# A fused diffusion-transformer step on one core: five fill groups ahead of the scan's first chunk in place of seven, and two 64-row copies that change engines

## The chip, the cores and the metric

One Trainium2 chip, one of its cores. The metric is the device time of one execution in microseconds (us), the median of several runs. Each of the core's engines works through its own queue of instructions in order: TensorE (PE in the profile; its weight loads are PEld), VectorE (DVE), ScalarE (ACT), GpSimd (POOL) and SyncE (SP), which issues all the DMA transfers of this kernel. They wait for each other by semaphores.

## The reference

One layer over 128 context tokens and 2048 latent tokens of width 1024, in 17 tiles of 128 tokens: a modulated RMSNorm; one projection; on one half of the heads a gated DeltaNet scan in both directions, on the other half a gMLP (gelu, layer norm, spatial mixing); an output projection with a gated residual; then a squared-ReLU MLP and a final norm. The part around the change is the scan with its triangular solve:

```python
a_mat = jnp.where(strict, jnp.einsum('bnhcd,bnhsd->bnhcs', k_beta, k) * decay, 0.0)
sol = lax.linalg.triangular_solve(a_mat + jnp.eye(DN_CHUNK), rhs, left_side=True, lower=True, unit_diagonal=True)

def step(S, xs):
    qd, kd, u_c, w_c, qk_c, gl = xs
    v_new = u_c - jnp.einsum('bhck,bhkv->bhcv', w_c, S)
    o = jnp.einsum('bhck,bhkv->bhcv', qd, S) + jnp.einsum('bhcs,bhsv->bhcv', qk_c, v_new)
    S = S * jnp.exp(gl)[..., None, None] + jnp.einsum('bhck,bhcv->bhkv', kd, v_new)
    return S, o
```

beside it `proj = h @ w_in`, of which the columns of the gate (g), of u and of vg (v) are computed here while the scan runs.

## The kernel before, in words

The program has three stages. The first projects q, k and v for all tiles and writes them to DRAM. The second, which the change touches, is the scan: 34 units (17 tiles, two directions), each a chunk of 128 tokens and four heads. The third is the MLP as one long row of matmuls.

In the scan each unit has a **prep** and a **chain**. The prep inverts a triangular matrix for four heads: a decay mask E (L1017, L1018 on ACT, two selections on POOL), the matrix KK (L1030 on DVE), its half-precision form AH (L1038 on ACT), a first X (L1039 on DVE), X transposed into Y (L1045 on PE, copied by L1047 on ACT). Then five levels of block size 2, 4, 8, 16, 32 follow. A level is a strict sequence over three engines: PE multiplies AH with Y (L1065), DVE copies the product under a mask into P (L1069), PE multiplies with P (L1076, L1079), ACT copies the new Y and X (L1080, L1081), and the next level can begin. The level of 64 rows is written apart: L1095 on PE, a copy Pm (L1097), L1103 and L1105 on PE, and the two copies Y (L1106) and X (L1107). L1113 and L1114 (PE) then read Y, their result goes through DVE into R (L1116), and L1122 (PE) reads X and R. The chain (L992, L1138, L1146, L1168, L1179, L1180) carries the state from unit to unit.

Since each prep step waits for the one ahead of it on another engine, PE is kept busy with **fills** between the steps. Fills are the 51 groups (17 tiles, g, v and u) of the second projection: a group is 24 matmuls of 128x512 (L224, L225, L226: a product in three parts over eight k), cut by `PARTS` into pieces of 9, 9 and 6 matmuls, followed by its gelu or gate on ACT and DVE (L1214 to L1274). The gate of a tile from the fifth on writes a buffer `gw` of which there is one, and stores it to DRAM (L1246); the next writer of `gw` waits for that store. Later fills are the output projection and the first norm of the MLP (L863 is an eviction of that norm on ACT).

The order is set by hand: every step is given a time in units of chunks by `at`, the list `p2` (the first eight numbers of `WINDOWS`) says how far ahead of unit i its prep runs (from i - 2.46 to i - 0.03), where its chain lies, and between which times the fills of the second projection are spread (`p2[4]` to `p2[5]`). The first `NF` groups are not spread: they are put at time -12 or -8, ahead of the prep of the first unit. The steps are sorted by time and written out; within limits a scheduler then orders the instructions of each engine.

At times between -2 and -1.2 `split_next` also splits the weights of u into two parts (L195 on ACT, L196 on DVE), eight tiles that are loaded four at a time.

Of the kernel before, what the change touches and what calls it, by code (L numbers as in the profile page):

```python
# [31 lines left out]
def interleave(*lists):  # L32
# [5 lines left out]
    for _, _, _, s in sorted(order, key=lambda e: e[:3]):  # L38
# [8 lines left out]
NE = 4  # L47
LAG2 = 0
LAG3 = 3
NF = 7  # L50
LATE = 0.5
PARTS = ((0, 3), (3, 6), (6, 8))
PL = 0
# [5 lines left out]
NK = DFF // P // 2  # L59
AHEAD = 3  # L60
COMPUTE = (mybir.EngineType.DVE, mybir.EngineType.Activation, mybir.EngineType.Pool)
WINDOWS = [2.46, 0.03, -0.51, 1.06, -1.61, 18.16, 17.58, 18.3,
           2.63, -0.06, -0.18, 1.0, 1.36, 1.64, 1.66, 2.66, 3.17, 3.71]


# [1 line left out]
def hybrid_step(  # L67
# [7 lines left out]
    V, A, G, T = nc.vector, nc.scalar, nc.gpsimd, nc.tensor  # L75
# [209 lines left out]
    with ExitStack() as ph:  # L285
# [478 lines left out]
        for bi in range(len(BLOCKS)):  # L764
# [8 lines left out]
            for n, (gi, h) in enumerate(order):  # L773
                u = us[n] if bi == 0 and n < 3 else feature_tile(blk, bi, gi, h)
# [156 lines left out]
    with ExitStack() as ph:  # L931
# [8 lines left out]
        def pd():  # L940
            return psd.tile([P, 4, P], F32, tag="d", name="pd", bufs=4)
# [40 lines left out]
        def unit(t, d, fresh=False, last=False):  # L982

            u = {}
# [28 lines left out]
            @prep.append  # L1013
            def _():
                e = s32("E")
                for h in range(H):
                    A.activation(e[:, h, :], u["gb"][:, h, :], AF.Abs, scale=-1.0, bias=col(gcol, h))  # L1017
                A.activation(e, e, AF.Exp, scale=-1.0)  # L1018
                es = s32("Es")
                G.affine_select(out=es, in_=e, pattern=[[0, 4], [-sg, P]], compare_op=ALU.is_gt, fill=0.0,  # L1020
                                base=0, channel_multiplier=sg)
                G.affine_select(out=e, in_=e, pattern=[[0, 4], [sg, P]], compare_op=ALU.is_ge, fill=0.0,
                                base=0, channel_multiplier=-sg)
                u["Es"], u["E"] = es, e
# [64 lines left out]
            ra, rb = (lo, hi) if d == 0 else (hi, lo)  # L1089
# [9 lines left out]
            @prep.append  # L1099
            def _():  # L1100
                py, px = pd(), pd()
                for h in range(H):
                    T.matmul(py[ra, h, 0:64], u["X"][ra, h, ra], u["P"][ra, h, 0:64], start=True, stop=True)  # L1103
                for h in range(H):
                    T.matmul(px[rb, h, 0:64], u["P"][ra, h, 0:64], u["X"][ra, h, ra], start=True, stop=True)  # L1105
                V.tensor_copy(u["Y"][ra, :, rb], py[ra, :, 0:64])  # L1106
                A.copy(u["X"][rb, :, ra], px[rb, :, 0:64])  # L1107

            @prep.append
            def _():  # L1110
# [193 lines left out]
        def split_next(j):  # L1304
            n, k = wlist[j]
            if n != "u" and k == 0:
                ga1.append(wrow(mod_d[1:2, 2 * D + n * 512 : 2 * D + n * 512 + 512]))
                WO.append([])
            (W2 if n == "u" else WO)[n].append(split_w(wraw[j]))
            ahead()  # L1310
# [83 lines left out]
        def at(time, fn, kind=None):  # L1394
            events.append((time, len(events), fn, kind))
# [20 lines left out]

        p2, p3 = WINDOWS[:8], WINDOWS[8:]
        for i, u in enumerate(units):
# [35 lines left out]
        for key, _, st in flat:  # L1454
            if key < NF * KT:
                at(-8 if key >= HT * KT else -12, st)
# [4 lines left out]
        for j in range(len(wlist)):  # L1461
            at(-2 + 0.12 * j if j < KT else 16.4 + 0.12 * (j - KT), lambda j=j: split_next(j))
        flat = [e[1:] for e in flat if e[0] >= NF * KT]
        done, total = 0, sum(size for size, _ in flat)
# [440 lines left out]
    for p, (o, n, m) in enumerate(seq):  # L1905
        u = units[n]
# [117 lines left out]
```

## Time and profile before

| | |
|---|---|
| runs of the kernel before | 2613.35, 2617.05, 2619.66 us; median 2617.05 us |
| the profiled execution's own time | 2613.28 us |
| its span, first to last instruction | 2611.1 us |
| TensorE busy | 2563.6 us, 98% of the span |
| VectorE, ScalarE, GpSimd busy | 1765.4, 1242.2, 255.2 us |
| the scan's stage | from about 433 to 1242 us of the span |

The busy time of an engine says how full it is. Where TensorE is 98% busy, what is left to gain is its idle time and the time in which it runs at a lower granted clock (the column PEclk). In a list of waits, each row names the waiting instruction by engine, tile and line, then what ended the wait, then the sum in us, the number of waits and the longest. In the timeline a row is a start, a duration, engine, line, operation, and in brackets the idle time ahead of it with what ended it.

### The profile page before, as it was taken

Reading aid. Unit: us, or ns where it says so; the run is one execution under the profiler, and the core shown is the slowest. Engines: PE = TensorE matmul, PEld = TensorE weight load, DVE = VectorE, ACT = ScalarE, POOL = GpSimd, SP = SyncE. Lnnn points to the kernel's source line nnn. Section 1 sums busy time; section 2 is a strip of 40 time slices with the busy share of each in tenths; the row PEclk is TensorE's granted clock in tenths of the full one; section 3 lists DMA queues with packets and bytes.
Section 4 is the critical chain, followed back from the end, with each engine's and each line's share of the span. In section 5 each row is a group of like instructions: output and inputs, shape, how many; then the busy total and the mean of one; then the engine's idle time right before and its main releaser. Section 6 shows DMA issues by size and latency. Waiting matters only on the chain.

```text
span 2611.1 us, 44100 instructions
## 1 busy us (share of the span) xinstructions
PE 2563.6 (98%) x15330; PEld 2151.3 (82%) x15330; DVE 1765.4 (68%) x3587; ACT 1242.2 (48%) x3086; POOL 255.2 (10%) x478
## 2 busy tenths in 40 slices
PE   8999999899999999999999999999999999999998
PEld 4999999788888778878888888888887888888887
DVE  5867745666566777886588786677675544774874
ACT  4755555455555667774345653333342432242441
POOL 3112112111111122221000000000000000000000
PEclk9999999999999999999999999999999999999999
DMA  8967638645555667995778788445379978786773
GB/s 295 291 214 219 197 113 240 214 146 164 156 158 169 212 198 239 282 299 163 289 228 243 242 253 319 150 126 162 108 209 382 339 259 289 257 254 211 233 254 106
DMA packets 533860, 579.78 MB, mean 222 GB/s; under 512 B 35500, under 2 KB 366684, under 8 KB 530054
## 3 DMA queue, kind: packets, MB, share of 16 engines
q1 hardware_dynamic: 533638, 576.98, 69.4%
q8 instruction: 120, 1.97, 0.3%
q14 instruction: 102, 0.84, 0.1%
HBM read 397.62 MB, written 179.22 MB: 221 GB/s over the span
## 4 chain that ended last, share of the span: by engine, by line
PE 89%; DMA 4%; DVE 3%; ACT 2%; issue 1%; SPq 0%; POOL 0%; DVEq 0%; POOLq 0%; ACTq 0%
PE f L224 17%; PE f L226 16%; PE f L225 16%; PE pj L224 7%; PE pj L226 7%; PE pj L225 7%; PE pd L992 3%; PE pm L224 2%; PE pm L225 1%; PE pm L226 1%; PE pm L339 1%; PE pt L593 1%; PE pd L1179 1%; PE pd L1180 1%; PE pt L553 1%
## 5 line engine op out<-in xcount | busy, mean ns | idle before, releaser
L224 PE MATMUL f<-hop,zH 128*128 128x512 f32 x960 | 373.7, 390 | 2.0 <-ACT zH L1527 2.0
L226 PE MATMUL f<-hop,zL 128*128 128x512 f32 x960 | 373.6, 390 | 0.0
L225 PE MATMUL f<-hop,zH 128*128 128x512 f32 x960 | 373.2, 389 | 0.0
L224 PE MATMUL f<-hop,wH 128*128 128x512 f32 x896 | 351.5, 393 | 0.0
L225 PE MATMUL f<-hop,wH 128*128 128x512 f32 x896 | 348.9, 390 | 0.0
L226 PE MATMUL f<-hop,wL 128*128 128x512 f32 x896 | 344.0, 390 | 0.0
L1527 ACT CAST zH<-zraw 128x512 fp32r<-128x512 f32 x240 | 146.7, 620 | 282.5 <-DVE zraw L1521 86.1
L224 PEld LDWEIGHTS f<-hop,zH 128*128 128x128 f32 x960 | 180.2, 188 | 40.3 <-ACT zH L1527 3.2
L226 PEld LDWEIGHTS f<-hop,zL 128*128 128x128 f32 x960 | 180.2, 188 | 39.0 <-DVE zL L1521 1.6
L225 PEld LDWEIGHTS f<-hop,zH 128*128 128x128 f32 x960 | 180.2, 188 | 37.2
L1521 DVE TENSOR_TENSOR zL<-zraw,zH 128x512 fp32r<-128x512 f32 x240 | 162.4, 687 | 71.6 <-ACT zH L1527 54.6
L226 PEld LDWEIGHTS f<-hop,wL 128*128 128x128 f32 x896 | 168.2, 188 | 35.7
L224 PEld LDWEIGHTS f<-hop,wH 128*128 128x128 f32 x896 | 168.5, 188 | 34.2 <-issue 0.9
L225 PEld LDWEIGHTS f<-hop,wH 128*128 128x128 f32 x896 | 168.6, 188 | 32.2
L226 PE MATMUL pj<-kH,wL 128*128 128x386 f32 (+2 forms) x568 | 190.5, 335 | 0.0
L224 PE MATMUL pj<-kH,wH 128*128 128x386 f32 (+2 forms) x568 | 189.1, 335 | 0.3 <-DVE kH L491 0.3
L225 PE MATMUL pj<-kL,wH 128*128 128x386 f32 (+2 forms) x568 | 189.4, 333 | 0.0
L182 POOL TENSOR_TENSOR r<-rsq,nhalf 128x1 f32<-128x1 f32 (+1 forms) x38 | 22.8, 600 | 1386.2 <-DVE rsq L181 1386.2
L1674 ACT CAST wH<-s 128x512 fp32r<-128x512 f32 x96 | 58.9, 620 | 170.9 <-DVE s L1521 157.6
L1069 DVE CAST_PREDICATED P<-om,pd 128x256 f16<-128x256 uint16 x170 | 71.9, 427 | 99.7 <-PE pd L1065 99.4
L541 DVE SCALAR_TENSOR_TENSOR cv<-pj,vec,cv 128x384 f32<-128x384 f32 (+2 forms) x164 | 87.1, 539 | 56.2 <-ACT cv L538 54.9
L224 PEld LDWEIGHTS pj<-kH,wH 128*128 128x128 f32 x568 | 107.1, 189 | 4.6 <-issue 4.2
(410 smaller groups left out, 5871.1 us busy)
## 6 DMA issues: line engine op xcount, KB each, us to landing
zraw<-z_d SPq DMA_DIRECT2D x212, 256.0 KB, 4.5
raw<-in_w_ff_dram SPq DMA_DIRECT2D x128, 256.0 KB, 4.9
hop<-hop_d SPq DMA_DIRECT2D x28, 1024.0 KB, 14.0
z_d<-c SPq DMA_DIRECT2D x96, 256.0 KB, 2.5
zraw<-s_d SPq DMA_DIRECT2D x96, 256.0 KB, 5.2
raw<-in_w_mod_dram SPq DMA_DIRECT2D x80, 256.0 KB, 4.4
r<-in_w_ff_dram SPq DMA_DIRECT2D x80, 256.0 KB, 5.5
s_d<-s SPq DMA_DIRECT2D x64, 256.0 KB, 3.0
```

Source lines behind the costliest of these rows:

```text
L224: T.matmul(ps, lh, rh, start=first and i == 0, stop=False, skip_group_check=more)
L225: T.matmul(ps, lh, rl, start=False, stop=False, skip_group_check=more)
L226: T.matmul(ps, ll, rh, start=False, stop=last and i == n - 1, skip_group_check=more)
L339: T.matmul(pm[0:2, :], scond[:, k, :], raws[k], start=k == 0, stop=k == KT - 1)
L541: V.scalar_tensor_tensor(out=cv[:, o : o + m], in0=ps[:, s + sh : s + sh + m], scalar=convw[:, w, j : j + 1], in1=cv[:, o : o + m], op0=AL ...
L553: T.transpose(pq[:, i * P : (i + 1) * P], u["x2"][:, i * P : (i + 1) * P], ident)
L593: T.matmul(ps[:, i * P : (i + 1) * P], kTt[:, i * P : (i + 1) * P], rhs[:, i * P : (i + 1) * P], start=True, stop=True)
L992: T.matmul(p[:, h, :], lhs[:, h, :], rhs[:, h, :], start=True, stop=True)
L1069: V.copy_predicated(out=half(u["P"], yi), mask=half(bc4(om[s]).bitcast(U16), yi), data=pp)
L1521: V.tensor_tensor(out=out, in0=a, in1=b, op=op)
L1527: A.copy(h, src)
L1674: A.copy(h, s2)
```

## The change

`NF` goes from 7 to 5: ahead of the first unit stand the groups g of tiles 0 to 3 and of tile 4, and no longer g of tile 5 and v of tile 4, which become spread fills. The fills are spread from -2.1 in place of -1.61; their end (18.16) stays. And the two copies of the 64-row level change engines: Y goes from VectorE to ScalarE, X from ScalarE to VectorE. The work is the same, instruction for instruction.

```diff
-NF = 7
+NF = 5
...
-WINDOWS = [2.46, 0.03, -0.51, 1.06, -1.61, 18.16, 17.58, 18.3,
+WINDOWS = [2.46, 0.03, -0.51, 1.06, -2.1, 18.16, 17.58, 18.3,
            2.63, -0.06, -0.18, 1.0, 1.36, 1.64, 1.66, 2.66, 3.17, 3.71]
...
                 for h in range(H):
                     T.matmul(px[rb, h, 0:64], u["P"][ra, h, 0:64], u["X"][ra, h, ra], start=True, stop=True)
-                V.tensor_copy(u["Y"][ra, :, rb], py[ra, :, 0:64])
-                A.copy(u["X"][rb, :, ra], px[rb, :, 0:64])
+                A.copy(u["Y"][ra, :, rb], py[ra, :, 0:64])
+                V.tensor_copy(u["X"][rb, :, ra], px[rb, :, 0:64])
```

**Start of the scan on TensorE.** The first rows of unit 0, before:

```order
L226 MATMUL pj<-wH,hL 128x512
L1045 LDWEIGHTS X
L1045 MATMUL pd<-ident_179,X 128x128
...
L1065 LDWEIGHTS AH
L1065 MATMUL pd<-Y,AH 128x64
...
L1076 LDWEIGHTS X
L1076 MATMUL pd<-P_5734,X 128x64
```

and now, where `pm` is the product of group g of tile 5:

```order
L226 MATMUL pm<-wH,hL 128x512
L1045 LDWEIGHTS X
L1045 MATMUL pd<-ident_179,X 128x128
...
L224 MATMUL pm<-wH,hH 128x512
L225 MATMUL pm<-wL,hH 128x512
L226 MATMUL pm<-wH,hL 128x512
...
L1065 LDWEIGHTS AH
L1065 MATMUL pd<-Y,AH 128x64
```

Before, unit 0 goes from L1045 over L1065, L1076 and L1079 to the next L1065 with no fill in between, after all seven groups. Now 9 matmuls of the sixth group stand ahead of L1045, 9 behind it, 6 behind L1065, and then a piece of 9, 9 or 6 between each two steps of the first levels.

**Start of the scan on ScalarE and VectorE.** ScalarE from the first AH on, before:

```order
L1038 CAST AH<-KK 128x512
L1244 ACTIVATE gw<-pm 128x512
L195 CAST wH<-raw 128x512
L1047 CAST Y<-pd 128x512
L1244 ACTIVATE gw<-pm 128x512
L195 CAST wH<-raw 128x512 x2
L1080 CAST Y<-pd 128x128x2
L1081 CAST X<-pd 128x128x2
```

and now:

```order
L1047 CAST Y<-pd 128x512
L195 CAST wH<-raw 128x512
L1080 CAST Y<-pd 128x128x2
L1081 CAST X<-pd 128x128x2
L195 CAST wH<-raw 128x512 x2
L1017 ACTIVATE E<-gr,gcol 128x128 x4
L195 CAST wH<-raw 128x512
L1080 CAST Y<-pd 128x64x4
L1081 CAST X<-pd 128x64x4
L1018 ACTIVATE E<-E 128x512
L1244 ACTIVATE gw<-pm 128x512
```

The second gate that writes `gw` (the second L1244) stood between L1047 and the first L1080; it now stands behind the second level's copies. VectorE at the same place, now:

```order
L1069 COPY_PREDICATED P_5734<-om_186,pd 128x128x2
L1068 COPY P_5734<-identq 128x512
L196 TENSOR_TENSOR wL<-raw,wH 128x512 x2
L1069 COPY_PREDICATED P_5735<-om_187,pd 128x64x4
```

Two splits of weights (L196) stand ahead of the mask copy of the second level (P_5735); before there was one between these two mask copies on a tile of the same load, and one on a tile loaded earlier.

**The 64-row copies.** VectorE in the 19th unit, before:

```order
L1215 TENSOR_SCALAR gw<-gw 128x512
L1083 TENSOR_TENSOR QK<-QK,E 128x512
L1039 TENSOR_TENSOR X<-AH,sg_185 128x512
L1048 TENSOR_TENSOR AL<-KK,AH 128x512
L1106 CAST Y<-pd 64x4x64
```

and ScalarE in the same unit now:

```order
L1097 CAST Pm<-pd 64x4x64
L195 CAST wH<-raw 128x512
L1214 ACTIVATE gw<-pm 128x512
L1038 CAST AH<-KK 128x512
L1106 CAST Y<-pd 64x4x64
```

Y stands on ScalarE in the place that X had there (behind L1038), and X on VectorE in the place that Y had (behind L1048). In the units of the backward direction in which the norm's evictions run (L863, eight to a unit), ScalarE had, before, in one of them:

```order
L863 ACTIVATE ev<-pj,b_203,a_202 128x128 x4
L1038 CAST AH<-KK 128x512
L863 ACTIVATE ev<-pm,b_203,a_202 128x128 x4
L1107 CAST X<-pd 64x4x64
```

and has now:

```order
L863 ACTIVATE ev<-pj,b_203,a_202 128x128 x4
L1038 CAST AH<-KK 128x512
L863 ACTIVATE ev<-pm,b_203,a_202 128x128 x2
L1106 CAST Y<-pd 64x4x64
L863 ACTIVATE ev<-pm,b_203,a_202 128x128 x2
```

so that two of the eight evictions moved from ahead of the copy to behind it.

## The prediction

> **What bounds the kernel now.** I read the page first: the engines' busy time and the chain that ended last.
>
> ```profile
> PE 2563.6 (98%) x15330; PEld 2151.3 (82%) x15330; DVE 1765.4 (68%) x3587; ACT 1242.2 (48%) x3086; POOL 255.2 (10%) x478
> PE 89%; DMA 4%; DVE 3%; ACT 2%; issue 1%; SPq 0%; POOL 0%; DVEq 0%; POOLq 0%; ACTq 0%
> ```
>
> TensorE is the bound, and it has 2611.1 - 2563.6 = 47.5 us of idle time in all. The change removes no matmul, so it can gain only idle time and time at a low clock. The windows say where these lie (PE busy is the second number, PEclk the one ahead of the DMA share):
>
> ```profile
> 450.00:475.00 25.00, 21.95 (x109) 17.85 (x108) 7.16 (x14) 6.72 (x15) 1.92 (x3) 0.99 1.06 347
> 475.00:500.00 25.00, 21.68 (x155) 16.41 (x154) 15.24 (x45) 13.88 (x37) 3.88 (x5) 0.88 0.52 154
> sum 720.00, PE 700.08 PEld 579.80 DVE 501.17 ACT 420.50 POOL 124.39; mean PE 29.17 PEld 24.16 DVE 20.88 ACT 17.52 POOL 5.18
> ```
>
> The two stretches of 25 us at the scan's start hold 3.05 + 3.32 = 6.4 us of idle time, and 12% of the second is clock that was not granted. The sum is that of 600 to 1320 us: 19.9 us idle over the rest of the scan. The list of waits of TensorE over 430 to 1250 us names them:
>
> ```profile
> PE pd L1076 <- DVE P L1069: 12.9, 18, 2.2
> PE pd L1065 <- ACT Y L1080: 4.8, 6, 2.7
> PE pd L1113 <- DVE Y L1106: 4.5, 4, 2.2
> ```
>
> These are the largest of 27.8 us; all are prep steps that had too few fills ahead of them. The mean of a wait at L1076 is 12.9/18 = 0.72 us.
>
> **Term 1, the start of the scan.** TensorE's timeline there, and the three rows of its waits from 470 to 500 us:
>
> ```profile
> 470.64 0.39 PE L226 MATMUL pj<-wH,hL 128*128 128x512 f32 x1
> 470.87 0.40 PE L1045 MATMUL pd<-ident,X 128*128 128x128 f16 x4
> 471.94 0.28 PE L1065 MATMUL pd<-Y,AH 128*128 128x64 f16 x4 [0.67 <-ACT Y L1047]
> 472.75 0.28 PE L1076 MATMUL pd<-P,X 128*128 128x64 f16 x4 [0.53 <-DVE P L1069]
> 475.86 0.37 PE L1065 MATMUL pd<-Y,AH 128*128 128x64 f16 x4 [2.71 <-ACT Y L1080]
> 476.62 0.63 PE L225 MATMUL pj<-wL,hH 128*128 128x512 f32 x1
> 477.05 0.63 PE L226 MATMUL pj<-wH,hL 128*128 128x512 f32 x1
> 481.35 0.40 PE L226 MATMUL pj<-wH,hL 128*128 128x512 f32 x1
> ...
> PE pd L1076 <- DVE P L1069: 3.0, 3, 2.2
> PE pd L1065 <- ACT Y L1080: 2.7, 1, 2.7
> PE pd L1065 <- ACT Y L1047: 0.7, 1, 0.7
> ```
>
> The waits add up to 6.4 us. Behind the longest the clock halves: matmuls follow each other at 0.43 us (476.62, 477.05) where the full clock gives 0.228 (a group of 24 in 5.46 us). From 475.86 to about 481.1 us stand 10 of these and three sets of four small ones (some 0.12 each): 5.2 us for 2.6 us of work, so 2.6 us lost. The start costs 6.4 + 2.6 = 9.0 us.
>
> What the long wait hung on stands in the other queues (ScalarE, VectorE, SP, a piece of the chain); behind them are the groups by line over 430 to 1250 us, with the mean in ns, and one more row of ScalarE:
>
> ```profile
> 473.92 0.60 ACT L1244 ACTIVATE gw<-pm 128x512 f32<-128x512 f32 x1 [2.03 <-DMA gate_d<-gw]
> 475.44 0.37 ACT L1080 CAST Y<-pd 128x256 f16<-128x256 f32 x1
> 461.11 0.41 DVE L1039 TENSOR_TENSOR X<-AH,sg 128x512 f16<-128x512 f16 x1
> 463.75 1.07 SPq L188 DMA_DIRECT2D raw<-in_w_in_dram  x2
> 467.23 0.52 SPq L1004 DMA_DIRECT2D kT<-kT_d  x1
> 468.01 5.83 DMA gate_d<-gw
> ...
> L195 ACT CAST wH<-raw 128x512 fp32r<-128x512 f32 x31 | 18.8, 626 | 2.1 <-DMA raw<-in_w_in_dram 1.5 <-PE pm L226 0.5
> L196 DVE TENSOR_TENSOR wL<-raw,wH 128x512 fp32r<-128x512 f32 x32 | 21.8, 690 | 5.1 <-ACT wH L195 4.6 <-PE pm L226 0.4
> L1069 DVE CAST_PREDICATED P<-om,pd 128x256 f16<-128x256 uint16 x170 | 71.9, 427 | 99.7 <-PE pd L1065 99.4
> 497.20 1.28 ACT L1017 ACTIVATE E<-gr,gcol 128x128 f32<-128x128 f32 x4
> ```
>
> The second gate waits for the store of the one `gw` buffer (issued at 468.01, landed 5.83 us later), and L1080 is queued behind it on ScalarE. The order of the change puts that gate behind the second level's copies.
>
> Now the changed order, walked with these durations. Of the 48 matmuls that move, 9 stay ahead of L1045 and 39 go behind it, so TensorE reaches L1045 at 470.87 - 39 x 0.228 = 462.0, and X is ready at 461.5: no wait. L1045 takes 0.23 on the queue and 9 matmuls 2.05, which covers the copy to Y (0.6): L1065 at 464.3 without a wait. Six matmuls (1.37) cover the mask copy (0.43): L1076 at 465.8. Nine cover L1080 (0.37, now with one cast ahead of it that is done early): L1065 at 468.2. Nine more: L1076 at 470.4. Here **something else is late**. The mask copy of the second level now stands behind two weight splits whose tiles SP issues at 463.75 and about 464.3. By the 5.83 us from issue to landing they come at 469.5 and 470.1; each costs a cast on ScalarE (0.6) and a subtraction on VectorE (0.69), so the second is through at 471.5 and the mask copy at 471.9: a wait of 1.5 us. Next, ScalarE has four L1017 (1.28 for four) and a cast of the third tile ahead of the second L1080. That load now stands in SP's queue in the place of the kT load (467.23), so it lands at 473.0; cast and copy end at 474.0, while TensorE would be at L1065 at 473.6: a wait of 0.4. The steps behind these have 6 to 9 matmuls in front (1.37 to 2.05 us) and their engines free: 0.2 for all. I add one more open place at the mean of 0.72. **Left: 2.8; gain 9.0 - 2.8 = 6.2 us.** No idle stretch there is near the 4 us that stood before the half clock, so I leave no half clock in. Bounds: 9.0 if the loads land sooner than needed; 0 if they land 2 to 3 us later, since then the idle stretch and the half clock come back.
>
> On the clock, the Trainium skill (TensorE: Matmul & The Clock Gate, Part 1) says the clock halves after an idle window of about 3.4 us and comes back after a busy one as long. The 4 us of waits above agree; the second dip, in the next term, follows 2.4 us (1168.43 to 1170.83) that hold only eight small matmuls, so here the trace shows it sooner. By the page the left waits would be further from a dip; by the row they have some 0.9 us of room. The sum is the same by both.
>
> **Term 2, the 64-row copies.**
>
> ```profile
> L1106 DVE CAST Y<-pd x34: 405/422/429, 500.1 to 1234.2; 64x256 f16<-64x256 f32 x34
> L1107 ACT CAST X<-pd x34: 353/367/380, 500.1 to 1234.2; 64x256 f16<-64x256 f32 x34
> 903.91 0.36 ACT L1107 CAST X<-pd 64x256 f16<-64x256 f32 x1
> 905.80 0.43 DVE L1106 CAST Y<-pd 64x256 f16<-64x256 f32 x1
> 990.32 1.53 ACT L863 ACTIVATE ev<-pm,b,a 128x128 f32<-128x128 f32 x4
> 1168.76 0.36 ACT L1107 CAST X<-pd 64x256 f16<-64x256 f32 x1 [1.27 <-PE pd L1105]
> 1168.43 0.19 PE L1105 MATMUL pd<-X,Pm 64*64 64x64 f16 x1
> 1168.92 0.28 PE L1076 MATMUL pd<-P,X 128*128 128x64 f16 x4 [0.29 <-DVE P L1069]
> 1170.34 0.43 DVE L1106 CAST Y<-pd 64x256 f16<-64x256 f32 x1
> 1170.83 0.27 PE L1113 MATMUL pd<-Y,AH 128*128 128x128 f16 x1 [1.51 <-DVE Y L1106]
> 1170.00:1175.00 5.00, 4.17 (x33) 4.16 (x32) 3.49 (x7) 0.56 (x2) 0.00 (x0) 0.66 0.84 255
> ```
>
> L1113 needs Y at once; X is read only by L1122, at least 2 us later in each of the 34 units. In all 34 ScalarE's X copy was done before L1113 began. At the three longer waits it was done earlier than VectorE's Y copy by 1.65 to 2.85 us (906.23 against 904.27 at the longest, 1170.77 against 1169.12 at the last). With Y in X's place L1113 waits 0.2 or less: of 2.2, 0.6 and 1.5 us come back 1.95, 0.6 and 1.5. **Gain 4.1 us**, from 0 to the 4.5 of the row of waits. X now comes late on VectorE, but R, which L1122 also reads, is made on VectorE behind it, so X adds 0.42 us there at most, under those 2 us. The five units with hardly any fill ahead of L1113 are the same five in both orders. Behind the last of these waits the clock falls to 0.66 over 5 us, 1.7 us lost; without the wait I take **1.5 us** of it as gained (0 to 1.7).
>
> A sentence of the Trainium skill speaks against this edit: ScalarE: Activation LUTs, Rules for kernel authors, puts cheap element-wise operations (relu, max, add, multiply) on VectorE rather than ScalarE, and a copy is of that kind. The rows differ, 367 ns on ScalarE and 422 on VectorE for this shape, and the place in the queue counts for more than either. By the page's order of the two the gain of 4.1 would shrink by the difference, some 0.06 us at each place.
>
> **Term 3, the rest of the scan.** The denser fills reshuffle all prep steps. Counting on TensorE's queue the prep steps with under 1 us of matmuls in front of them, behind the first 30 us and without L1113, I find 23 before and 22 now. At 0.72 each that is no change: 0, between -3.6 and +3.6 (five places more or fewer). Behind the scan TensorE is busy without a break, so what is gained arrives at the end.
>
> **Sum.** 6.2 + 4.1 + 1.5 + 0 = 11.8 us. The profiled execution took 2613.28 (its span and 2.2 around it) and would take 2601.5. The median of the runs shown, 2617.05, is 3.8 above it; I take the gain off the median: **2605.3 us**, 0.45% less.
>
> **Rivals.** (A) *The start stays starved.* The loads in front of the scan keep the DMA engines full (share 1.06 in the first window quoted), and the splits now stand between two mask copies. If the tiles land at 472 or later, the wait at the second level is 3.5 to 4 us and the clock halves: 9.0 - (4 + 2.6 + 1.3) = 1.1 gained, 6.7 in all, and nothing of the clock in term 2: 5.2, so 2611.8. For it speaks that both engines are blocked by the same loads; against, that the landing is measured. (B) *Y takes ScalarE's queue as its new wait, slower.* In eight backward units the copy stands behind evictions (L863, 1.53 us for four), and in four of these the X copy ended only 0.18 us before L1113. If ScalarE runs four evictions late there, each unit loses 1.53 - 0.18 = 1.3 us, 10.8 in all, with one more half clock (2.6); against the 6.2 of the start that is 7.2 slower: 2624. It decides once the copy ends more than some 1 us later against L1113 than X does now. Against it: the new order moves up to two evictions behind the copy. (C) *Only the start gains*, since L1122 then waits for X on VectorE as long as L1113 did for Y: 6.2, so 2610.9. Against it are the 2 us and more between L1113 and L1122.
>
> **How the numbers follow.** Forecast 0.60, A 0.16, C 0.12, B 0.07, other 0.05. A measurement tells 0.2%, 5.2 us, from no change: faster is under 2611.8, slower over 2622.3. Faster: nearly all of the forecast (0.57), half of A (0.08), two thirds of C (0.08), 0.01 of the others: 0.74. Slower: B and a little: 0.08. Same: 0.18. The best corner is 9.0 + 4.5 + 1.7 + 3.6 = 18.8, so 2598; the range goes from 2598 to 2615, over A and C and short of B.
>
> **What would show it.** In the profile after: L1045 of the first unit near 462 us with no wait; a wait of 1 to 2 us at the second level's L1076, put down to DVE; PEclk 1.00 in every window from 460 to 500 us and from 1150 to 1180; no wait of L1113 over 0.5 us; waits of TensorE in the scan near 20 us in place of 28. It is wrong if the second level waits over 3 us or the clock dips there (A), if L1113 waits for ACT (B) or L1122 for DVE (C), or if the waits at L1076 and L1065 behind 520 us add up to 4 us more than now, which would be term 3 and not the edits.

## The result, and the profile after

| | this kernel, median us (lowest to highest) | kernel before, same chip | ratio, 95% interval |
|---|---|---|---|
| changed kernel, first measurement | 2607.9 (2606.41 to 2611.17) | 2614.45 | 0.9977 (0.9968 to 0.9987) |
| changed kernel, second measurement | 2609.2 (2603.74 to 2611.75) | 2614.25 | 0.9983 (0.9975 to 0.9992) |

The change makes the kernel 0.17 to 0.23% faster, 5 to 6.5 us. 2605.3 was forecast, 11.8 us less than the 2617.05 shown; the median of the kernel before turned out 2.6 us lower than those three runs had it. So the direction and the range held, and about half of the gain did not arrive. The rest of this text is about that half.

The list of waits of TensorE over 430 to 1250 us, after (sum in us, number, longest):

```profile
PE pd L1076 <- DVE P L1069: 14.2, 18, 3.2
PE pd L1065 <- ACT Y L1080: 3.2, 7, 0.8
...
PE pd L1113 <- ACT Y L1106: 0.9, 4, 0.4
```

L1113 has gone from 4.5 to 0.9 and L1065 from 4.8 to 3.2, but L1076 from 12.9 to 14.2, with a new longest wait of 3.2. (The lists put some waits of L1076 down to another VectorE line, L1335 or L1338: 2.2 us before, 1.2 now. By all rows L1076 went from 15.1 to 15.4.) Windows say where (after the length: busy us of PE, PEld, DVE, ACT, POOL; PEclk; DMA share; GB/s):

```profile
475.00:500.00 25.00, 22.87 (x185) 17.57 (x185) 18.96 (x55) 14.96 (x41) 6.42 (x7) 1.00 0.59 194
1110.00:1140.00 30.00, 26.76 (x219) 22.22 (x217) 20.07 (x47) 19.65 (x59) 6.45 (x8) 0.89 0.82 253
1170.00:1200.00 30.00, 29.84 (x267) 24.30 (x267) 24.05 (x60) 18.81 (x62) 5.69 (x6) 1.00 0.82 254
1131.00:1137.00 6.00, 5.98 (x28) 4.96 (x28) 2.63 (x7) 2.35 (x8) 0.00 (x0) 0.50 0.48 147
```

The start runs at the full clock now and TensorE does 185 matmuls from 475 to 500 us where it did 155; the dip of 1170 to 1175 is gone. In their place stands a hole at 1110 to 1140, where the kernel before had none:

```profile
1110.00:1140.00 30.00, 29.43 (x262) 24.17 (x261) 25.40 (x64) 24.67 (x74) 7.83 (x9) 1.00 0.95 281
```

It is 3.24 us of idle time, and then 6 us at half the clock (the last row of after), 3 us lost. The start itself, on TensorE's timeline:

```profile
462.67 0.40 PE L1045 MATMUL pd<-ident,X 128*128 128x128 f16 x4
472.51 0.28 PE L1076 MATMUL pd<-P,X 128*128 128x64 f16 x4 [1.01 <-DVE P L1069]
475.21 0.28 PE L1065 MATMUL pd<-Y,AH 128*128 128x64 f16 x4 [0.83 <-ACT Y L1080]
481.75 0.40 PE L1045 MATMUL pd<-ident,X 128*128 128x128 f16 x4 [1.57 <-DVE X L1039]
```

And the hole, over four queues (SP, VectorE, TensorE, a piece of the chain of waits):

```profile
1117.61 1.08 DVE L1378 TENSOR_TENSOR x<-x,tmp 128x512 f32<-128x512 f32 x1
1117.96 0.67 SPq L1327 DMA_DIRECT2D ob<-ob_d  x1
1118.67 1.86 SPq L1349 DMA_DIRECT2D x<-in_x_sample_dram  x2
1120.91 0.33 SPq L1380 DMA_DIRECT2D x_d<-x  x1
1120.91 6.29 DMA x_d<-x
1127.23 0.49 DVE L853 TENSOR_SCALAR x<-x,r 128x512 f32<-128x512 f32 x1 [3.15 <-DMA x_d<-x]
1130.54 0.43 DVE L1069 CAST_PREDICATED P<-om,pd 128x256 f16<-128x256 uint16 x1
1131.02 0.37 PE L1076 MATMUL pd<-P,X 128*128 128x64 f16 x4 [3.24 <-DVE P L1069]
```

L1378 has made the second half of x at 1118.69. Its store (L1380) is issued 2.2 us later, since in SP's queue the loads of `ob` and of two halves of `x` stand ahead of it, and lands 6.29 us after that. Not all of the 2.2 us is issuing: by SP's own list of waits it waited 0.7 us for the load `eg` to land ahead of the second `x`, and 0.3 for `kt` ahead of the store. L853, the scaling of the norm, writes over the tile that is being stored, so it waits for the landing, 3.15 us; VectorE works in order, and behind L853 stand L1138, L1377, L1378, four short instructions and then the mask copy L1069 that TensorE needs. Neither the prediction nor its rivals had this chain.

### The profile page after: what moved, and what is told of

It reads as the page before. It is cut to its first block, busy times and chain, and to the rows that moved or that the text cites. A ratio compares the mean times of both kernels' runs of the same rounds, so it can differ in the third digit from the quotient of the medians.

```text
span 2608.3 us, 44097 instructions
## 1 busy us (share of the span) xinstructions
PE 2563.6 (98%) x15330; PEld 2148.5 (82%) x15330; DVE 1771.7 (68%) x3587; ACT 1245.5 (48%) x3086; POOL 257.9 (10%) x478
## 4 chain that ended last, share of the span: by engine, by line
PE 54%; DMA 5%; DVE 3%; ACT 2%; issue 1%; SPq 0%; DVEq 0%; POOLq 0%; POOL 0%; ACTq 0%
PE f L224 15%; PE f L225 15%; PE f L226 15%; PE pj L224 2%; PE pj L226 2%; PE pj L225 2%; DMA r<-in_w_ff_dram 1%; PE pd L992 1%; DMA x_d<-x 1%; DMA x<-x_d 1%; DMA traw<-in_w_ff_dram 1%; DMA zraw<-z_d 1%; PE pd L1179 0%; PE pd L1180 0%; DMA hop_d<-opL 0%
## 5 line engine op out<-in xcount | busy, mean ns | idle before, releaser
L224 PE MATMUL f<-hop,zH 128*128 128x512 f32 x960 | 373.6, 390 | 1.5 <-ACT zH L1527 1.4
L224 PE MATMUL f<-hop,wH 128*128 128x512 f32 x896 | 351.7, 393 | 1.0 <-ACT wH L1674 1.0
L224 PEld LDWEIGHTS f<-hop,zH 128*128 128x128 f32 x960 | 180.2, 188 | 40.0 <-ACT zH L1527 2.8
L224 PEld LDWEIGHTS f<-hop,wH 128*128 128x128 f32 x896 | 168.5, 188 | 35.8 <-ACT wH L1674 1.8
L224 PE MATMUL pj<-kH,wH 128*128 128x386 f32 (+2 forms) x568 | 189.2, 336 | 0.8 <-DVE cv L541 0.5
L1069 DVE CAST_PREDICATED P<-om,pd 128x256 f16<-128x256 uint16 x170 | 72.2, 429 | 89.2 <-PE pd L1065 89.0
L224 PEld LDWEIGHTS pj<-kH,wH 128*128 128x128 f32 x568 | 107.1, 189 | 5.4 <-issue 5.0
## 6 DMA issues: line engine op xcount, KB each, us to landing
hop<-hop_d SPq DMA_DIRECT2D x28, 1024.0 KB, 11.7
```

The lines of the kernel that those rows point to most:

```text
L224: T.matmul(ps, lh, rh, start=first and i == 0, stop=False, skip_group_check=more)
L1069: V.copy_predicated(out=half(u["P"], yi), mask=half(bc4(om[s]).bitcast(U16), yi), data=pp)
```

## The experiments

Each is compared with the kernel before on the same chip; the runs were made on two chips, so that between runs the ratios compare better than the medians. The theory formed from the two traces: the fills gain what was forecast; the exchange of the copies moves a store behind three loads in SP's queue, and VectorE, waiting for that store, gives the gain back. The rivals are stated run by run.

| run | median us | kernel before, us | ratio, 95% interval |
|---|---|---|---|
| changed kernel again | 2609.2 | 2614.25 | 0.9983 (0.9975 to 0.9992) |
| fills only | 2604.9 | 2614.25 | 0.9966 (0.9954 to 0.9978) |
| copies only | 2613.65 | 2614.25 | 1.0001 (0.9992 to 1.0010) |
| changed, scaling apart | 2600.9 | 2614.25 | 0.9954 (0.9941 to 0.9966) |
| the same again | 2599.9 | 2615.2 | 0.9938 (0.9925 to 0.9952) |
| before, scaling apart | 2612.55 | 2613.7 | 1.0001 (0.9992 to 1.0010) |
| fills only, scaling apart | 2603.1 | 2613.7 | 0.9968 (0.9956 to 0.9979) |
| changed, store by GpSimd's queue | 2605.2 | 2615.2 | 0.9960 (0.9948 to 0.9973) |
| scaling apart, splits later | 2603.4 | 2613.7 | 0.9967 (0.9955 to 0.9979) |
| scaling apart, not stretched | 2604.7 | 2613.7 | 0.9966 (0.9952 to 0.9979) |
| scaling apart, both copies on ScalarE | 2601.5 | 2615.2 | 0.9946 (0.9934 to 0.9959) |
| scaling apart, half the splits on GpSimd | 2598.9 | 2615.2 | 0.9941 (0.9929 to 0.9954) |

**The changed kernel again.** No edit.

> The changed kernel once more, unchanged. Its first profile has one wait of TensorE that the profile before does not have: 3.24 us at L1076 near 1131 us, put down to VectorE's mask copy L1069, with the clock at about half for 6 us behind it. Theory (the wait belongs to the order): VectorE's scaling L853 overwrites a tile of x whose store SP issues late, so L853 waits some 3 us for the DMA and the mask copy stands behind it; the profile taken again shows the same wait of 2 to 4 us within 3 us of that place, and PEclk below 0.95 in the window 1110 to 1140. Rival (an accident of one execution, a late landing): no wait over 1 us there and PEclk 1.00, and the profiled execution is some 6 us shorter than the first, near 2604. Time by both: ratio to the kernel before 0.997 to 0.998.

The timelines of VectorE and of TensorE in this execution:

```profile
1126.07 0.49 DVE L853 TENSOR_SCALAR x<-x,r 128x512 f32<-128x512 f32 x1 [2.67 <-DMA x_d<-x]
1129.86 0.28 PE L1076 MATMUL pd<-P,X 128*128 128x64 f16 x4 [2.75 <-DVE P L1069]
1130.41 0.40 PE L225 MATMUL pm<-wL,oH 128*128 128x512 f32 x1
```

The wait is there again at the same instruction, 2.75 us, so it belongs to the order. The half clock does not: the next matmul takes 0.40, where the first profile had 0.63, and this execution (2606.8 us) was 3.5 us shorter than the first (2610.3). The expectation of a clock below 0.95 failed.

**Fills only, copies only.** Each takes one part of the change.

```diff
 # fills only: the changed kernel with
-A.copy(u["Y"][ra, :, rb], py[ra, :, 0:64])
-V.tensor_copy(u["X"][rb, :, ra], px[rb, :, 0:64])
+V.tensor_copy(u["Y"][ra, :, rb], py[ra, :, 0:64])
+A.copy(u["X"][rb, :, ra], px[rb, :, 0:64])
 # copies only: the kernel before with this turned round
```

> Only the fill groups change (five groups ahead of the scan, spread from -2.1); the 64-row copies stay as before, Y on VectorE and X on ScalarE. Theory (the fills gain at the start and cost nothing later; the lost time near 1131 us comes from the copies, which move the store x_d<-x behind three loads in SP's queue): the start gains 5 to 6 us, the three longer waits at L1113 stay with their sum of 4 to 5 us, no wait over 1 us within 5 us of 1131: about 5.5 us less than before (ratio 0.9979), so as fast as the whole change or within 1 us of it. Rival 1 (the lost time near 1131 us comes from the denser fills): the wait of 3 us is here too and the time equals that of the kernel before within 1.5 us (ratio 0.9995 to 1.0005). Rival 2 (the start gains nothing that arrives at the end): also equal to before, but with no wait near 1131 us.

> Only the two 64-row copies change engines; seven groups ahead of the scan as before. Theory: L1113's waits fall from 4.5 us to under 1 and the clock dip near 1171 us goes (3.7 + 1.5 gained), but the store x_d<-x now stands behind three loads in SP's queue as in the whole change; if the scaling L853 waits for it as long as there, 3.2 us and the half clock (together some 6 us) are lost near 1135 us, so the time is that of before within 2 us (ratio 0.999 to 1.001). Rival 1 (that loss comes from the denser fills): 5 us less than before, ratio 0.998, with no wait over 1 us near 1135 us. Rival 2 (the Y copies wait in ScalarE's queue): L1113 waits for ACT in several units, over 3 us in all, and the time is above before.

The fills alone take 0.34% off, more than the whole change (2604.9 against 2609.2 us, run side by side, though the intervals of the ratios overlap); the copies alone take nothing off. In the fills-only kernel, the list of waits of TensorE over 430 to 1250 us, then the same over 455 to 500:

```profile
PE pd L1076 <- DVE P L1069: 6.7, 13, 1.0
PE pd L1113 <- DVE Y L1106: 5.1, 5, 2.1
...
PE pd L1076 <- DVE P L1069: 1.2, 2, 0.9
PE pd L1045 <- DVE X L1039: 1.0, 1, 1.0
PE pd L1065 <- ACT Y L1080: 0.2, 1, 0.2
```

and its SP and VectorE queues at the place of the hole:

```profile
1115.78 0.85 DVE L1378 TENSOR_TENSOR x<-x,tmp 128x512 f32<-128x512 f32 x1
1116.66 0.32 SPq L1380 DMA_DIRECT2D x_d<-x  x1
1121.47 0.62 SPq L1327 DMA_DIRECT2D ob<-ob_d  x1
1121.62 0.88 DVE L853 TENSOR_SCALAR x<-x,r 128x512 f32<-128x512 f32 x2
1123.76 0.45 DVE L1069 CAST_PREDICATED P<-om,pd 128x256 f16<-128x256 uint16 x1
```

With Y on VectorE the store is issued as soon as L1378 ends, ahead of `ob` and `x`, and L853 runs both halves without a wait. With Y on ScalarE it stands behind them, with seven fill groups as with five. The copies-only kernel has the hole too, and its half clock (0.63 for one matmul a microsecond later):

```profile
PE pd L1076 <- DVE P L1069: 17.4, 22, 2.5
PE pd L1113 <- ACT Y L1106: 1.0, 4, 0.5
...
1138.24 0.28 PE L1076 MATMUL pd<-P,X 128*128 128x64 f16 x4 [2.55 <-DVE P L1069]
1139.29 0.63 PE L224 MATMUL pm<-wH,oH 128*128 128x512 f32 x1
```

So L1113 gained 3.5 us and the row of L1076 lost 4.5 (17.4 against 12.9). By all rows L1076 lost 2.3 (17.4 against 15.1) and TensorE's waits in the scan fell from 27.8 to 26.5 us, but this profile has less clock at the start (0.82 over 475 to 500 us, against 0.88 before), and the time is the same. Both expectations of the theory held, and rival 1, that the fills bring the hole, fell. One number was too small: the fills gained 9 us where 5.5 were expected.

**The scaling apart.** L853 writes to two free buffers and not over the tile that is stored.

```diff
 def scale2():
-    for n in range(2):
-        V.tensor_scalar_mul(u["x"][n], u["x"][n], u["r"])
+    for n, o in enumerate(own_x() if own_x else list(u["x"])):
+        V.tensor_scalar_mul(o, u["x"][n], u["r"]); u["x"][n] = o
 # in the scan: own_x gives a tile of tag "vg" and one of tag "gw"
```

> The changed kernel, in which the scaling L853 of the first norm writes to two other tiles (the free buffers of vg and gw) and no longer over the tile that is being stored, so it need not wait for the store x_d<-x; the schedule behind 960 us shifts a little with it. Theory (the rest of the gain is lost where VectorE waits for this store): L853 waits for no DMA (10.5 us in six places now), the wait of 3.24 us at L1076 near 1131 us and the half clock behind it are gone, and the time is 4 to 6 us below the changed kernel, ratio to before 0.9955 to 0.996. Rival (the wait moves to the next thing in that unit, since TensorE is short of fills there): a wait of 2 us or more stays within 5 us of that place, and the time is that of the changed kernel within 1.5 us (ratio 0.997 to 0.998).

> The run with the scaling apart once more, as the measure for the three beside it. Theory: ratio to before 0.995 to 0.996 as the first time, with no wait over 1 us between 1100 and 1150 us. Rival (the first was a good day): 0.9965 or more.

> The kernel before, with the scaling L853 writing to two other tiles, so that it need not wait for the store x_d<-x (6.6 us in five places before). Theory: there the store stands ahead of the three loads in SP's queue and the mask copy further ahead in VectorE's, so the waits of L853 hardly reach TensorE: 0 to 2.5 us less than before, ratio 0.999 to 1.000. Rival (waiting for the store costs TensorE as much in the kernel before as in the changed one, so that the scaling apart is an improvement of its own and says nothing on the change): 5 to 8 us less, ratio 0.997 to 0.998.

In the changed kernel this takes 8 us off (2609.2 to 2600.9) where 4 to 6 were expected, in the kernel before nothing, though L853 waited there too (6.6 us in five places). With the fills alone it takes nothing off either (0.9966 without it, 0.9968 with it, further below). Waiting for the store is thus not a cost by itself; it became one when the exchange put the store late and the mask copy close behind. The rows of the profile of the first such kernel, its waits and its mask copy at the place of the hole:

```profile
PE pd L1076 <- DVE P L1069: 11.0, 19, 1.5
PE pd L1113 <- ACT Y L1106: 0.8, 4, 0.3
...
1126.53 0.28 PE L1076 MATMUL pd<-P,X 128*128 128x64 f16 x4 [0.30 <-DVE P L1069]
```

2.75 us of wait have become 0.30. All waits of TensorE over 430 to 1250 us were 23.2 and 21.3 us in the two profiles of the changed kernel and are 19.1 and 17.4 in the two of this one, some 4 less, and the half clock that followed the wait in one of two profiles is worth 3; together 4 to 7 of the 8 us. The rest I did not find in a row. The edit also moves the order: in this kernel the second L853 stands behind the mask copy, and the store behind `ob` and one half of `x`, 1.5 us after its data. So this run does not separate the wait from the new order; the next one leaves the scaling as it was.

**The store through another queue.** The scaling stays in place, and the store leaves SP's queue.

```diff
-store(out=x2_d[t * P : (t + 1) * P, sl], in_=x)
+nc.gpsimd.dma_start(out=x2_d[t * P : (t + 1) * P, sl], in_=x)
```

> The changed kernel (scaling in place as it was), with the store x_d<-x issued from GpSimd's queue in place of SP's, so that it does not stand behind the loads of ob and x; the schedule behind 980 us shifts with it. Theory (L853 waits so long since SP issues the store 2.2 us after its data are ready, behind three loads of which each also fills the DMA engines): the store is issued within 1 us of L1378's end, L853 waits under 1.5 us at each place, no wait of L1076 over 1.5 us near 1130 us, and the time is 3 to 7 us below the changed kernel, ratio 0.9955 to 0.9972. Rival (the landing itself, 5 us and more while the DMA engines are full, is what counts): L853 still waits 2 us or more somewhere and the time is that of the changed kernel, ratio 0.9975 to 0.9985.

```profile
1115.32 1.42 DVE L1378 TENSOR_TENSOR x<-x,tmp 128x512 f32<-128x512 f32 x1
1117.15 0.61 POOL L1380 DMA_DIRECT2D x_d<-x  x1 [0.96 <-DVE X L1107]
1121.23 0.96 DVE L853 TENSOR_SCALAR x<-x,r 128x512 f32<-128x512 f32 x2
DVE x L853 <- DMA x_d<-x: 7.2, 7, 1.5
```

Issued 0.4 us after its data, the store no longer holds L853 at that place, the longest wait for it is 1.5 us, and the kernel is 10 us faster than before (0.9960). The stores did not land sooner in this run (2.3 to 7.3 us after the issue, median 4.6; in the changed kernel 2.0 to 6.1, median 3.1, where the trace gives it): the place in SP's queue counts, not the landing alone (the order behind 980 us shifts in this kernel too, so it is not that place alone). The sum of L853's waits is still 7.2 us, which supports that only the one at the wrong place counts.

**What the exchange is worth without the store.** Fills and scaling apart, copies as before.

> Five fill groups spread from -2.1 and the scaling L853 apart, but the 64-row copies as before (Y on VectorE, X on ScalarE); against the run with all three it prices the copies alone, without the store in their way. Theory (the copies are worth their waits at L1113, some 4 us): L1113 waits 4 to 5 us, the time is 3 to 5 us above the run with all three, ratio to before 0.966 of one per cent below: 0.9966 to 0.9974. Rival (the Y copy only moves the wait, to L1122 or to the next step): L1113's waits are there but others are shorter, and the time is that of the run with all three within 1.5 us, ratio 0.995 to 0.996.

2603.1, against 2600.9 and 2599.9 with the exchange: the exchange is worth 2 to 3 us by the medians, or 3 to 5 with each taken against its own kernel before; the interval of the ratio overlaps with that of the first of these and not with that of the second. By the waits L1113 has 6.0 in place of 0.8, but L1076 6.9 in place of 11.0, so most of what L1113 gains comes back at L1076. Where, the timeline of the changed kernel (second block) shows against the fills-only kernel (first block), with VectorE's share of the 15 us around it (the fourth number of the row of a window), each from its own profile:

```profile
897.57 0.22 PE L1113 MATMUL pd<-Y,AH 128*128 128x128 f16 x1 [2.11 <-DVE Y L1106]
893.00:908.00 15.00, 12.31 (x114) 9.93 (x113) 14.18 (x44) 8.28 (x20) 3.03 (x3) 1.00 0.77 240
```

```profile
909.06 0.28 PE L1076 MATMUL pd<-P,X 128*128 128x64 f16 x4 [1.17 <-DVE P L1069]
912.98 0.28 PE L1076 MATMUL pd<-P,X 128*128 128x64 f16 x4 [0.99 <-DVE P L1069]
895.00:910.00 15.00, 13.41 (x127) 11.09 (x126) 14.13 (x44) 10.45 (x27) 4.17 (x5) 1.00 0.69 224
```

VectorE is busy 14.2 of 15 us in both. TensorE no longer waits 2.11 at L1113 (0.42 is left), and waits 1.17 + 0.99 = 2.16 at the next two steps that need VectorE. Two equal copies changed places, so VectorE's backlog is the same, and TensorE meets it two steps later.

**Does taking work off VectorE help there?** Two kernels, both with the scaling apart.

```diff
 # both copies on ScalarE
-V.tensor_copy(u["X"][rb, :, ra], px[rb, :, 0:64])
+A.copy(u["X"][rb, :, ra], px[rb, :, 0:64])
 # half the splits on GpSimd: L196 of every second tile of the output weights
-V.tensor_tensor(out=lo, in0=raw, in1=f32(h), op=ALU.subtract)
+(eng or V).tensor_tensor(out=lo, in0=raw, in1=f32(h), op=ALU.subtract)
```

> The run with the scaling apart, and both 64-row copies on ScalarE (Y, then X), none on VectorE. From 897 to 912 us VectorE is busy 14.26 of 15 us, and the 2.2 us that L1113 no longer waits stand there as 1.17 + 0.99 at the next two L1076. Theory (the wait at L1113 was VectorE's backlog; the exchange of two equal copies left that backlog as it was and only moved the place where TensorE meets it): with 0.41 us less on VectorE in each unit the two waits of 2.16 us shrink by 0.4 to 0.8, all of L1076 from 11 to 8 to 10 us, and the time falls by 0.5 to 2 us against the run with the scaling apart (which runs beside it again). Rival (the waits at L1076 come from X on ScalarE or from the order of the queue alone): L1076's waits stay within 0.5 of 11 us, or waits on ACT grow by over 1 us, and the time is the same or higher.

> The run with the scaling apart, and of the 16 weight splits of the output projection, which fall between 870 and 915 us, every second subtraction (L196) on GpSimd in place of VectorE, so some 5.5 us less for VectorE there. Theory (VectorE's backlog is what TensorE waits for between 880 and 935 us: 0.82, 1.17, 0.99 and 0.78 at L1076): these four waits fall from 3.8 us to under 1.5, and the time by 2 to 3 us against the run beside it, ratio to before 0.9942 to 0.995. Rival (GpSimd, which makes Es, E and KK of the next unit, becomes late in its place, or the steps have too few fills anyway): the waits there stay at 3 us or more, at L1045 and L1065 among others, and the time is the same within 1 us or higher.

The two waits of 2.16 shrank as the theory said, to 0.88 + 0.58 with both copies on ScalarE and 0.48 + 0.53 with the splits halved. But right behind them TensorE now waits for ScalarE, where it did not before. With both copies on ScalarE:

```profile
908.21 0.28 PE L1076 MATMUL pd<-P,X 128*128 128x64 f16 x4 [0.88 <-DVE rr L1338]
912.11 0.50 PE L224 MATMUL pm<-wH,oH 128*128 128x512 f32 x1 [0.52 <-ACT oH L1357]
```

That makes 1.98 in place of 2.16, and 1.45 with the splits halved (0.24 at L1065 and 0.20 at L224 beside the two). Nor did VectorE empty: from 897 to 912 us it is busy 14.3 and 14.2 of 15 us, and 14.3 in the run beside them, so the work that went made room for other work. The time did not follow (2601.5 and 2598.9, against 2599.9 for the run beside them), and neither did TensorE's waits in the whole scan: 18.9 us in both, 17.4 in the run beside them. In the first, L1045 waits 1.0 us more for the first X on VectorE, and L1076 0.7 more at 506 us and 0.55 more at 1126; in the second a wait of 0.66 stands at L1076 at 898, and 0.84 and 0.78 stay at 890 and 932, so the four waits that were to fall from 3.8 to under 1.5 us came to 2.6. The rivals held for the time: these two runs did not make the kernel measurably faster, and since VectorE stayed as full as it was, they do not show what a smaller backlog would be worth.

**The start.** Two edits of numbers, with the scaling apart.

```diff
 # splits later
-at(-2 + 0.12 * j if j < KT else ...)
+at(-1.8 + 0.12 * j if j < KT else ...)
 # not stretched
-WINDOWS = [2.46, 0.03, -0.51, 1.06, -2.1, 18.16, ...
+WINDOWS = [2.46, 0.03, -0.51, 1.06, -1.61, 18.16, ...
```

> The run with the scaling apart, and the weight splits of u (L195, L196) 0.2 of a chunk later (from -1.8), which takes one of two splits from ahead of the second level's mask copy. Theory (the waits left at the scan's start hang on these splits and their late tiles): of the 4.4 us of waits between 455 and 500 us 1.5 to 3 go, and the time falls by as much, ratio to before 0.9943 to 0.995. Rival (TensorE is short of fills there, the wait only moves to the next level or to the fills of u that need these weights): waits of 4 us or more stay up to 510 us and the time is the same within 1 us, ratio 0.995 to 0.996.

> The run with the scaling apart, but the fills are spread from -1.61 again with five groups ahead of the scan: the first unit's L1045, L1065 and L1076 have no fill between them, the later levels have 9, 9 and 6. Theory (the gain at the start comes from the fills that stand between the first steps): waits of 0.5 us at the first L1065 and L1076 come back and a wait of 1 to 3 us at the next L1065, with the half clock behind it if the three come close together: the time is 2 to 5 us above the run it is made from, ratio to before 0.9962 to 0.9974. Rival (it is enough that the two gates and the splits no longer stand together; five groups do that): within 1 us of the run it is made from, ratio 0.995 to 0.996.

Later splits did not help: the wait at the second level's L1076 goes, as was expected, but the waits at the start rise from 4.4 to 6.1 us (2.15 at L1065, 1.92 at the second unit's L1045, 0.92 and 1.09 at L1076), and the time is 2.5 to 3.5 us above the run that it is made from (the interval of the ratio overlaps with that of its first measurement, not of its second). My theory for the rest at the start failed; the rival held. Without the stretch the first steps stand together again:

```profile
461.58 0.40 PE L1045 MATMUL pd<-ident,X 128*128 128x128 f16 x4 [1.86 <-DVE X L1039]
462.65 0.28 PE L1065 MATMUL pd<-Y,AH 128*128 128x64 f16 x4 [0.67 <-ACT Y L1047]
463.73 0.37 PE L1076 MATMUL pd<-P,X 128*128 128x64 f16 x4 [0.80 <-DVE P L1069]
464.83 0.37 PE L1065 MATMUL pd<-Y,AH 128*128 128x64 f16 x4 [0.51 <-ACT Y L1080]
450.00:475.00 25.00, 21.15 (x113) 0.86 1.08 355
```

3.84 us of waits within some 5 us and a clock of 0.86 in that window (the longest stands ahead of L1045, not at the next L1065 as was expected, and 2.06 us more follow at L1076 at 493): 2604.7, 4 to 5 us above. It is the fills between the first steps that bring the start's gain, not the gates and splits being apart.

## Why the prediction was right, and where it was wrong

**Term 1, the start: right.** 6.2 was predicted from 9.0 of loss with 2.8 left. After, 3.7 are left (1.01 at the second level's L1076 and 0.83 at L1065, which were named as 1.5 and 0.4; 1.57 at the second unit's L1045, which was not; 0.28 more) and no half clock: 5.3. L1045 stands at 462.67 where 462.0 was worked out, and the steps behind it come within 1.2 us of the times given. The run without the stretch confirms the cause, and with the splits later the wait at the second level's L1076, put down to two splits, is gone. Rival A, the starved start, did not come.

**Term 3, the rest of the scan: its sign was open, and the fills gained there.** The prediction took 0, from 23 thinly covered places before and 22 after. With the fills alone, L1076 behind the start fell from 12.9 - 3.0 = 9.9 to 6.7 - 1.2 = 5.5 us, 4.4 less (4.7 with the rows of L1335). With 6.6 at the start (6.4 of waits less 2.4, and the 2.6 of half clock) and L1113 0.6 up, that is about 10, against 9 measured. Counting places at a mean wait could not see it: the count of thin places hardly moved, but the waits that came of them fell from 15 to 11 and their mean from 0.66 to 0.50. Which of the moved fills brought that is open.

**Term 2, the 64-row copies: this is the step that failed.** It said that 4.1 us at L1113 come back, and 1.5 with the clock. L1113 went from 4.5 to 0.9, as the text worked out, but the gain of the exchange is nothing by itself (1.0001), and in company with the fills it takes back 3 to 4 us (0.9966 to 0.9977 and 0.9983; the intervals overlap, the medians run side by side are 4.3 apart). Three things were wrong in it. (a) "With Y in X's place L1113 waits 0.2 or less: of 2.2 ... come back 1.95" took the end of one wait for a gain; VectorE was full there (14.2 of 15 us), and TensorE met the same backlog at the next two L1076, 2.16 us. (b) The prediction costed the exchange as two copies and left out what else it moves. The schedule answered with another order on SP: the store L1380 behind `ob` and `x`, the mask copy behind L1377 and L1378; a wait of 2.75 and 3.24 us in the two profiles, once with 3 us of half clock. (c) The dip of 1.5 us was tied to the wait of 1.51 at L1113. The fills-only kernel and the kernel before with the scaling apart have that wait of 1.51 in the same sequence of matmuls, with PEclk 1.00 over the 30 us around it.

**The rivals.** B (the Y copy behind evictions on ScalarE) and C (L1122 waits for X) did not come: L1113 waits for ACT 0.9 us in four places, and L1122 is not among the waits listed in that profile. B saw the risk in the right edit but not the mechanism: the price of the exchange is paid on VectorE and SP, not on ScalarE.

**The signs named.** No wait of L1113 over 0.5 and a full clock at 460 to 500 and 1150 to 1180 came; 23.2 us of waits in the scan stand against "near 20". The mark for term 3 (4 us more at L1076 and L1065 behind 520) was not reached as a sum: their rows go from 11.7 to 14.9 us, 3.2 more, about the size of the new wait.

**What was luck.** The direction and the range held, but the sum did not come about as forecast: 5.3 at the start, about 4 in the rest of the scan where 0 was taken, and 3 to 4 lost by the exchange where 5.6 was to come. An unforecast gain covered an unforecast loss. The time itself, 2607.9 against 2605.3, looks only 2.6 us off because the median of before had been taken 2.6 us too high; in the gain the miss is 5.3 us (6.5 against 11.8).

## What to carry over

A wait that ends on a full engine is not all gained by serving it first: look at how busy that engine is over the 10 to 20 us around, and at the next instruction that needs it. When an edit changes the engine of an instruction and a scheduler decides the order, compare the queues of all engines along the whole stage, SP's too; the cost here stood 650 us behind the first place looked at. An operation that overwrites a tile while it is being stored ties an engine's in-order queue to a landing; a second buffer took 8 us off the changed kernel (and nothing off the kernel before, where the waits stood off TensorE's path), and the kernel with five groups, the exchange and the scaling apart (0.9938 to 0.9954) beats both kernels.

## What the runs showed of the hardware

The half clock does not follow from the length of a gap alone. These rows are one stretch, the same instructions with gaps alike within 0.1 us, in the kernel before (first block) and in the fills-only kernel (second): L1113 waits 1.51 us in both, and the next L1180 takes 0.63 in one and 0.39 in the other.

```profile
1170.83 0.27 PE L1113 MATMUL pd<-Y,AH 128*128 128x128 f16 x1 [1.51 <-DVE Y L1106]
1172.16 0.63 PE L1180 MATMUL pd<-vn,QK 128*128 128x128 f32 x2
```

```profile
1161.92 0.22 PE L1113 MATMUL pd<-Y,AH 128*128 128x128 f16 x1 [1.51 <-DVE Y L1106]
1162.64 0.39 PE L1180 MATMUL pd<-vn,QK 128*128 128x128 f32 x2
```

Likewise the wait of 3.24 us was followed by half the clock, that of 2.75 was not, and that of 2.55 was. So here a dip seen in one profile could not be counted as a term that an edit removes. The Trainium skill (TensorE: Matmul & The Clock Gate, Part 1) says that the gate watches a free-running window of about 3.4 us; that one stretch goes both ways agrees with a window that runs free, but a stretch of 2.4 us that halves the clock is shorter than the idle window the page names. No run here shows where the window lay.

In the changed kernel's first profile the 256 KB stores of L1380 landed 2.0 to 6.1 us after their issue where the trace gives it (median 3.1), and the one at the hole took 6.29 by the chain of waits, with the DMA engines at a share of 0.82 over 1110 to 1140 us and 1.03 over 1125 to 1131. The kernel before has one of 6.6 us too, so a long landing does not come from the place behind the loads alone. Issued from GpSimd's queue it took that engine 0.61 us, against 0.33 of SP.
